# Moving a context's keys and values for the second layer from beside a token layer to beside the experts

## The chip, the cores and the metric

The kernel runs on one core of a Trainium2 chip. The metric is the device time of one execution in microseconds (us), from the first to the last instruction plus a small constant around them. Smaller is better.

## What is computed

Two transformer blocks run one after the other over 256 tokens of width 1024, in 32-bit floats.

The first block is a recurrent and attention mixer, then a mixture of 32 experts (four per token, each expert 1024 x 2048 and 1024 x 1024). The second block has two layers over the same tokens and, beside them, 256 context vectors:

```python
for l in range(2):
    need_ctx = l < 1
    mod, modc = silu(c) @ w_mod[l] + b_mod[l], silu(c_ctx) @ w_mod[l] + b_mod[l]
    sh1, sc1, gt1, sh2, sc2, gt2 = split(mod, 6)          # csh1, csc1, ... from modc
    h  = rms_norm(xl, g_pre_mix[l]) * (1 + sc1) + sh1
    hc = rms_norm(xc, g_pre_mix[l]) * (1 + csc1) + csh1
    ...                      # tokens attend to keys and values of context and tokens
    xl = ...                 # mixer and gated feed-forward of the tokens
    if need_ctx:
        xc = ...             # the same for the context, in layer 0 only
```

So the context passes through layer 0 as a whole (its input does not depend on the first block), and in layer 1 only its keys and values are wanted: a norm, a modulation by `csc1` and `csh1`, and products with two 1024 x 1024 parts of `w_in[1]`.

## The kernel before

**Pieces.** Every weight matrix of a mixer or feed-forward is read in pieces of 128 x 2048 floats (1 MiB). A piece is split into a high and a low part in two halves (`split`, lines 393 and 394: a copy on ScalarE, a subtraction on VectorE), and multiplied in three products: `fm` (lines 414 to 416, weights stationary), `tm` (lines 437 to 439, activations stationary) and `tm2` (lines 463 to 465, two pieces at once). A piece whose inner size is 1024 is 48 matmuls with 256 moving columns. The pieces of `w_f2b` have an inner size of 768 and 36 matmuls each.

**Two paths.** The tokens' path writes its products to the PSUM tiles `ps_a` and `ps_b`, the context's path and the modulations to `ps_c`. Both are Python generators which yield after each piece; `drive(main, side, ratio)` takes `ratio` steps of the side for each step (or credit) that the main yields. This gives the written order. At build a scheduler orders the instructions of each engine anew, except where the code pins them, so the order that runs can differ from the written one. An engine runs its own list in order.

**Stages, in order of time.**
- The first block (`block1`, up to about 360 us), with the modulations as its side: `side_a` reads 1 MiB of modulation weights a step and multiplies (line 484). A modulation has three groups of eight steps; group 0 holds shift and scale of the mixer's norm. `RATIO_A` is the side's share. `hook`, after the merge of the first block, drains that side and begins the context's layer 0.
- The experts (`moe`): 12 sets, first four of four experts ("quads"), then six of two ("pairs"), then two of two ("mixed"). Each set yields 24 times. Its weights come by SyncE's queue into `raw`, its products are lines 1192 and 1217, its results are added by line 1236. The side is the context's layer 0, `CREDIT[n]` steps for each yield of a set with n experts. Its weights come by GpSimd's queue into `rawh`. `CTX_STEPS` counts all steps of that side, and `REST` of them are held back until the experts are done.
- `moe_rest`: the residual and the norm of the tokens. The steps held back (before: the last four pieces, of `w_f2b`) run beside it.
- The tokens' layer 0, with `side_c`: the modulation of layer 1 (24 steps), then `ctx_kv`, which norms the context's result (line 1348 loads it from `xcd` in DRAM, line 540 transposes it), multiplies eight pieces and writes keys and values to DRAM (`spill`).
- The tokens' layer 1, which has no side. Between two stages of a layer, `res_end` adds the residual and gets the factors of the norm (`nrx`), `transposed` (line 540) multiplies by a diagonal `dg`, and `norm_fm` writes `hh` and `hl`, which the next pieces read.

Of the kernel before, what the change touches and what calls it, by code (L numbers as in the profile page):

```python
# [28 lines left out]
for _s in SETS:  # L29
    for _r, _o, _m in _s:  # L30
        CAPS[_r] = _m
CREDIT = {1: 0.0, 2: 0.07, 4: 0.6}
NEG = 1e30
HEADS = 16
CONVW = 31
WINS = (2, 4, 8, 16)
RAW = 6
RATIO_C = 0.36

START_B = 3  # L40
PRE_B = (2, 0, 9)
PRE_C = (8,)
HOLD = 4
RATIO_A = 1.15

CTX_STEPS = 78
REST = 4


# [13 lines left out]
def _kt(h, l):  # L63

    return lambda k: (h[:, k, :], l[:, k, :])
# [147 lines left out]
def drain(gen):  # L213
    for _ in gen:
        pass
# [19 lines left out]
def drive(main, side, ratio):  # L235

    acc = 0.0
    for w in main:
        acc += ratio * w
        while acc >= 1.0:  # L240
            acc -= 1.0
            if next(side, None) is None:
                acc = 0.0
                break
# [60 lines left out]
class _Kernel:  # L305
# [864 lines left out]
    def experts(self, tp, rawp, es, rs, xg, b1, sel, ct, acc, mid=None, first=None):  # L1170
# [9 lines left out]
        parts.reverse()  # L1180
        credit = CREDIT[n]
        aT = tp.tile([128, 8, 128], F32, name="aT", tag="aT", bufs=1)
# [153 lines left out]
    def ctx_kv(self, p, l, x, mod):  # L1336

        A, V, S = self.A, self.V, self.S
        wi = A["w_in2"][l]
        mT = mod["T"][1]  # L1340
        with p.pool(f"kv{l}") as hp:
            Ax = hp.tile([128, 8], F32, name="Akv")
            V.scalar_tensor_tensor(Ax, mT[:, 8:16], 1.0, self.col(f"gpm{l}"), op0=OP.add, op1=OP.mult)
            hh = hp.tile([128, 8, 256], F32R, name="hh4")
            hl = hp.tile([128, 8, 256], F32R, name="hl4")
            with p.pool(f"kvn{l}") as np_:
                xs = np_.tile([128, 2, 1024], F32, name="xc3")
                self.nc.gpsimd.dma_start(xs, x)
                ss = np_.tile([128, 2], F32, name="ssk")
                self.row_ss(np_, xs, ss)  # L1350
                self.rstd_to(ss, ss, 2, 1024)
                self.norm_fm(np_, xs, ss, Ax, mT[:, 0:8], hh, hl)
            yield 1
            act = _kt(hh, hl)
            with p.pool(f"kvs{l}") as kp:
                for ch in range(4):
                    kc = kp.tile([128, 2, 256], F32, name="kc", tag="kc")
                    vc = kp.tile([128, 2, 256], F32, name="vc", tag="vc")
                    self.fm(p, wi[8 + ch], act, 8, lambda _, ps: S.activation(kc, ps, AF.Copy))
                    yield 1  # L1360
                    self.tm(p, wi[12 + ch], act, 8, lambda ps: S.activation(vc, ps, AF.Copy))
                    self.spill(l, ch, kc, vc)
                    yield 1
# [449 lines left out]
    def run(self, out):  # L1813
        nc, A, V = self.nc, self.A, self.V
        cp, dp = self.cp, self.dp
        x = cp.tile([128, 2, 1024], F32, name="x")
        nc.sync.dma_start(x, A["x"].rearrange("(a p) d -> p a d", p=128))
        self.ssx = cp.tile([128, 2], F32, name="ssx")
        self.nrx = cp.tile([128, 2], F32, name="nrx")
        self.modT = cp.tile([128, 48], F32, name="modT")  # L1820
        self.modg = dp.tile([128, 512], F32, name="modg")
        st1 = cp.tile([128, 8, 32], F32, name="st1")
        s1 = self.silu_cols(cp, self.col("c"), 8, "s1")
        V.tensor_copy(st1, s1[:, :, None].to_broadcast([128, 8, 32]))
        st2 = cp.tile([128, 8, 32], F32, name="st2")
        s2 = self.silu_cols(cp, self.col("c2"), 8, "s2")
        V.tensor_copy(st2[:, :, 0:16], s2[:, :, None].to_broadcast([128, 8, 16]))
        s3 = self.silu_cols(cp, self.col("cc2"), 8, "s3")
        V.tensor_copy(st2[:, :, 16:32], s3[:, :, None].to_broadcast([128, 8, 16]))
        mods = []  # L1830
        for l in range(2):
            mods.append(dict(g=dp.tile([128, 512], F32, name=f"mg{l}"),
                             T=[cp.tile([128, 48], F32, name=f"mT{l}{i}") for i in range(2)]))
        self.kvd = [[dp.tile([128, 2, 2, 256], F32, name=f"kvd{l}{ch}") for ch in range(4)] for l in range(2)]
        ctx = A["ctx"].rearrange("(a p) d -> p a d", p=128)

        def mod_steps(l):
            return self.mods(st2, l + 1, A["w_mod"][l], mods[l]["g"], mods[l]["T"], [0, 16])

        b1c = ExitStack()  # L1840
        self.gcols = self.gate_cols(b1c.enter_context(self.px.pool("b1c")))

        xT = self.rawp.tile([128, 2048], F32, name="raw", tag="raw").rearrange("p (k t) -> p k t", k=8)
        with self.px.pool("xn") as np_:
            self.row_ss(np_, x, self.ssx)
            self.rstd_to(self.nrx, self.ssx, 2, 1024)
            self.transposed(np_, x, self.nrx,
                            lambda a, k, pt: self.S.activation(xT[:, k:k + 4, a * 128:(a + 1) * 128], pt, AF.Copy))
        with b1c, self.px.pool("modp", 1) as self.modp:
            drain(self.mods(st1, 0, A["w_ada"], self.modg, [self.modT], [0], (0,)))  # L1850

            def side_a():
                yield from self.mods(st1, 0, A["w_ada"], self.modg, [self.modT], [0], (1, 2))
                yield from mod_steps(0)
            side = side_a()
            xcd = dp.tile([128, 2, 1024], F32, name="xcd")
            cside = _Steps(self.layer(self.pc, 0, ctx, mods[0], True, end=xcd), CTX_STEPS - REST)

            def hook():
                drain(side)  # L1860
                next(cside)
            drive(self.block1(x, xT, hook), side, RATIO_A)

        drive(self.moe(x), cside, 1.0)
        drain(cside)
        g2 = self.gain_row(self.rawp, self.modg, 2, 0, "raw")
        cside.limit = CTX_STEPS
        self.prefetch(self.pc, [A["w_f2b"][0][i] for i in range(4 - REST, 4)])
        self.prefetch(self.px, [A["w_in2"][0][ch] for ch in PRE_C])
        self.moe_rest(x, g2)  # L1870
        drain(cside)

        def side_c():
            yield from mod_steps(1)
            yield from self.ctx_kv(self.pc, 1, xcd, mods[1])
        with self.px.pool("modp2", 1) as self.modp:
            side = side_c()
            main = self.layer(self.px, 0, x, mods[0], False)
            next(main)
            cside.limit += 1  # L1880
            drain(cside)
            drive(main, side, RATIO_C)
            drain(side)
        self.px.score = ["b", "c"]
        drain(self.layer(self.px, 1, x, mods[1], False, end=out.rearrange("o (a p) d -> p (o a) d", p=128)))
# [17 lines left out]
```

## Time and profile before

| | |
|---|---|
| median of 3 runs | 2774.47 us (2771.18 to 2781.82) |
| the profiled execution | 2777.74 us |
| its span, first to last instruction | 2776.0 us |
| TensorE matmul busy | 2596.7 us (94%) |
| VectorE busy | 1442.4 us (52%) |
| ScalarE busy | 1097.5 us (40%) |
| moved by DMA | 790.96 MB, mean 285 GB/s |

The share of busy time is a mean over stages with different limits. Matmuls overlap, so the distance from one start to the next, not the mean duration of one, is what a matmul costs; a busy TensorE in a stretch means that its list was never empty there. A row of a stretch gives its borders (us from the span's start) and its length, then busy us and, in brackets, the number of instructions of TensorE's matmuls, its weight loads, VectorE, ScalarE and GpSimd (left out where there are none), then TensorE's granted clock as a share of the full one, the mean busy share of the 16 DMA engines, and GB/s. A row of the timeline gives start, length, engine, source line, operation, output and inputs, shapes, how many were merged, and in square brackets how long the engine stood idle before and what ended that.

### The profile page before, as it was taken

The numbers are of one execution on the slowest core, as the hardware profiler recorded it, in microseconds if no ns is written. First come the engines' busy times: TensorE is split into PE (matmuls) and PEld (weight loads), VectorE is DVE, ScalarE is ACT, GpSimd is POOL, SyncE is SP. The second block draws the span as 40 slices with busy tenths as digits, with TensorE's granted clock in tenths as the row PEclk, the third lists the DMA queues.
The fourth block names the chain that finished last, engine by engine and source line by source line (L and its number), as shares of the span: only waits on it lengthen the run. The fifth ranks groups of instructions, "written<-read, shape, count | busy, mean of one in ns | idle before, by whom it ended". The sixth has DMA issues, their size and how long they took to land. (4 is left out here: it accounts for less than half of the span.)

```text
span 2776.0 us, 47595 instructions
## 1 busy us (share of the span) xinstructions
PE 2596.7 (94%) x19078; PEld 1971.1 (71%) x19078; DVE 1442.4 (52%) x2413; ACT 1097.5 (40%) x1970; POOL 264.1 (10%) x436
## 2 busy tenths in 40 slices
PE   6999998998998999999898879999999999999998
PEld 4888875666666665553333258779899998899998
DVE  3974566733434333221111158786655658866655
ACT  3663444432323231211100035555543555556443
POOL 1100011112011110000000012210000022200000
PEclk8999999999999999999999989999999999999999
DMA  8768779999999999989999984446666453345452
GB/s 354 263 247 322 274 280 380 363 348 391 395 405 384 404 408 398 373 322 373 390 401 395 391 308 161 157 177 231 251 224 239 166 201 122 122 158 192 152 193 81
DMA packets 154912, 790.96 MB, mean 285 GB/s; under 512 B 17888, under 2 KB 19936, under 8 KB 96064
## 3 DMA queue, kind: packets, MB, share of 16 engines
q1 hardware_dynamic: 131824, 705.30, 66.9%
q0 software_dynamic: 22864, 82.59, 7.8%
q8 instruction: 151, 2.47, 0.3%
q14 instruction: 73, 0.60, 0.1%
HBM read 780.74 MB, written 7.08 MB: 284 GB/s over the span
## 5 line engine op out<-in xcount | busy, mean ns | idle before, releaser
L394 DVE TENSOR_TENSOR wl<-raw,wh 128x1024 fp32r<-128x1024 f32 (+1 forms) x410 | 497.2, 1218 | 293.1 <-ACT wh L393 291.0
L393 ACT ACTIVATE wh<-raw 128x1024 fp32r<-128x1024 f32 (+1 forms) x410 | 425.9, 1046 | 482.8 <-PE ps_a L415 311.4
L414 PE MATMUL ps_a<-hh,wh 128*128 128x256 f32 x1888 | 542.0, 287 | 6.6 <-ACT wh L393 3.1
L416 PE MATMUL ps_a<-hh,wl 128*128 128x256 f32 x1888 | 531.4, 282 | 0.5 <-DVE wl L394 0.5
L415 PE MATMUL ps_a<-hl,wh 128*128 128x256 f32 x1888 | 531.5, 282 | 0.1
L414 PEld LDWEIGHTS ps_a<-hh,wh 128*128 128x128 f32 x1888 | 358.6, 190 | 52.9 <-issue 37.2
L415 PEld LDWEIGHTS ps_a<-hl,wh 128*128 128x128 f32 x1888 | 358.6, 190 | 3.4 <-DVE hl L564 1.2
L416 PEld LDWEIGHTS ps_a<-hh,wl 128*128 128x128 f32 x1888 | 358.4, 190 | 2.9 <-DVE wl L394 2.5
L394 DVE TENSOR_TENSOR wl<-rawh,wh 128x1024 fp32r<-128x1024 f32 x132 | 161.9, 1227 | 320.4 <-ACT wh L393 299.7
L393 ACT ACTIVATE wh<-rawh 128x1024 fp32r<-128x1024 f32 x132 | 139.9, 1060 | 427.8 <-PE ps_c L415 242.0
L414 PE MATMUL ps_c<-hh,wh 128*128 128x256 f32 x832 | 238.4, 286 | 0.0
L416 PE MATMUL ps_c<-hh,wl 128*128 128x256 f32 x832 | 237.2, 285 | 0.0
L415 PE MATMUL ps_c<-hl,wh 128*128 128x256 f32 x832 | 236.8, 285 | 0.0
L1192 PE MATMUL ps_b<-raw,xg 128*32 128x512 f32 (+1 forms) x1152 | 181.4, 610 | 25.9 <-DMA raw<-in_w_dram 25.9
L1192 PE MATMUL ps_a<-raw,xg 128*32 128x512 f32 (+1 forms) x1152 | 184.9, 619 | 18.0 <-DMA raw<-in_w_dram 17.9
L414 PEld LDWEIGHTS ps_c<-hh,wh 128*128 128x128 f32 x832 | 157.8, 190 | 26.3 <-issue 23.4
L416 PEld LDWEIGHTS ps_c<-hh,wl 128*128 128x128 f32 x832 | 157.8, 190 | 16.6 <-issue 15.7
L415 PEld LDWEIGHTS ps_c<-hl,wh 128*128 128x128 f32 x832 | 157.6, 189 | 15.4 <-issue 15.4
L1715 DVE SCALAR_TENSOR_TENSOR wv<-u,cw,wv 128x256 f32<-128x256 f32 x360 | 166.6, 498 | 0.5
L1192 PEld LDWEIGHTS ps_b<-raw,xg 128*32 128x32 f32 (+1 forms) x1152 | 47.1, 120 | 126.2 <-issue 86.3
L1192 PEld LDWEIGHTS ps_a<-raw,xg 128*32 128x32 f32 (+1 forms) x1152 | 48.2, 121 | 121.8 <-issue 91.2
L1217 PE MATMUL ps_b<-raw,aT 128*32 128x512 f32 (+1 forms) x576 | 91.9, 615 | 10.0 <-DMA raw<-in_w_dram 10.0
(524 smaller groups left out, 4815.5 us busy)
## 6 DMA issues: line engine op xcount, KB each, us to landing
raw<-in_w_dram SPq DMA_DIRECT2D x384, 512.0 KB, 12.6
raw<-in_w_dram SPq DMA_DIRECT2D x192, 1024.0 KB, 8.5
raw<-in_w_in_dram SPq DMA_DIRECT2D x96, 1024.0 KB, 4.9
raw<-in_w_mod_dram SPq DMA_DIRECT2D x48, 1024.0 KB, 5.0
raw<-in_w_f_dram SPq DMA_DIRECT2D x44, 1024.0 KB, 4.8
raw<-in_w_ada_dram SPq DMA_DIRECT2D x24, 1024.0 KB, 8.3
rawh<-in_w_in_dram POOLq DMA_DIRECT2D x48, 512.0 KB, 7.6
rawh<-in_w_f_dram POOLq DMA_DIRECT2D x44, 512.0 KB, 7.7
```

The costliest lines, as they stand in the source:

```text
L393: s = self.S.activation(h[:, :n], src, AF.Copy)
L394: self.V.tensor_sub(l[:, :n], src, h[:, :n].bitcast(F32))
L414: self.T.matmul(o, wh[:, w], ah, start=(k == 0), stop=False)
L415: self.T.matmul(o, wh[:, w], al, start=False, stop=False)
L416: self.T.matmul(o, wl[:, w], ah, start=False, stop=(k == kt - 1))
L1192: T.matmul(ps[c], xg[:, k, c], ws[i][:, o:o + 512], start=False, stop=(k == 7), tile_position=(0, c.start))
L1217: T.matmul(py[h][c], aT[:, f, c], ws[i][:, h * 512:(h + 1) * 512], start=(f == 0), stop=(f == 7), tile_position=(0, c.start))
L1715: return V.scalar_tensor_tensor(wk, u[:, f, j:j + 256], cw[:, j * 4 + k:j * 4 + k + 1], wk, op0=OP.mult, op1=OP.add)
```

## The change

The modulation's group 0 of layer 1 is made at the end of the first block's side. The context's chain beside the experts no longer ends with its layer 0 but goes on with `ctx_kv`: 11 more steps, of which two are new yields before the norm. The four steps held back behind the experts are now the last four pieces of keys and values, and `w_f2b` runs beside the experts. Two-expert sets give 0.15 steps a yield for 0.07. The tokens' layer 0 keeps 16 steps of modulation as its side. `RATIO_A` and `RATIO_C` follow the new numbers of steps.

```diff
-CREDIT = {1: 0.0, 2: 0.07, 4: 0.6}
+CREDIT = {1: 0.0, 2: 0.15, 4: 0.6}
-RATIO_C = 0.36
+RATIO_C = 0.25
-RATIO_A = 1.15
-
-CTX_STEPS = 78
+RATIO_A = 1.38
+
+
+CTX_STEPS = 78 + 11
...
                 self.nc.gpsimd.dma_start(xs, x)
+                yield 1
                 ss = np_.tile([128, 2], F32, name="ssk")
                 self.row_ss(np_, xs, ss)
                 self.rstd_to(ss, ss, 2, 1024)
+                yield 1
                 self.norm_fm(np_, xs, ss, Ax, mT[:, 0:8], hh, hl)
...
-        def mod_steps(l):
-            return self.mods(st2, l + 1, A["w_mod"][l], mods[l]["g"], mods[l]["T"], [0, 16])
+        def mod_steps(l, gs=(0, 1, 2)):
+            return self.mods(st2, l + 1, A["w_mod"][l], mods[l]["g"], mods[l]["T"], [0, 16], gs)
...
                 yield from mod_steps(0)
+                yield from mod_steps(1, (0,))
             side = side_a()
             xcd = dp.tile([128, 2, 1024], F32, name="xcd")
-            cside = _Steps(self.layer(self.pc, 0, ctx, mods[0], True, end=xcd), CTX_STEPS - REST)
+
+            def ctx_chain():
+                yield from self.layer(self.pc, 0, ctx, mods[0], True, end=xcd)
+                yield from self.ctx_kv(self.pc, 1, xcd, mods[1])
+            cside = _Steps(ctx_chain(), CTX_STEPS - REST)
...
-        self.prefetch(self.pc, [A["w_f2b"][0][i] for i in range(4 - REST, 4)])
+        self.prefetch(self.pc, [A["w_in2"][1][c + ch] for ch in range(4 - REST // 2, 4) for c in (8, 12)])
...
-        def side_c():
-            yield from mod_steps(1)
-            yield from self.ctx_kv(self.pc, 1, xcd, mods[1])
         with self.px.pool("modp2", 1) as self.modp:
-            side = side_c()
+            side = mod_steps(1, (1, 2))
```

## Rows read from the trace of the kernel before

**Rows 1.** The page: TensorE, DMA share and DMA rate in 40 slices.

```profile
PE   6999998998998999999898879999999999999998
DMA  8768779999999999989999984446666453345452
GB/s 354 263 247 322 274 280 380 363 348 391 395 405 384 404 408 398 373 322 373 390 401 395 391 308 161 157 177 231 251 224 239 166 201 122 122 158 192 152 193 81
```

**Rows 2.** Busy time by stretch: first block, last quad, five sets, token layer 0.

```profile
45.00:300.00 255.00, 252.56 (x1990) 208.93 (x1993) 168.90 (x280) 136.33 (x255) 21.68 (x30) 1.00 0.79 291
...
902.40:1071.00 168.60, 158.08 (x1255) 114.82 (x1253) 64.00 (x74) 50.39 (x65) 19.37 (x36) 1.00 1.03 407
1071.00:1152.10 81.10, 81.10 (x456) 45.05 (x454) 22.78 (x33) 15.35 (x24) 4.97 (x10) 1.00 0.96 376
1152.10:1231.30 79.20, 79.20 (x440) 43.04 (x439) 21.52 (x33) 14.93 (x25) 1.80 (x4) 1.00 0.88 343
1231.30:1299.50 68.20, 61.48 (x285) 24.79 (x283) 11.69 (x23) 7.11 (x16) 0.74 (x2) 0.97 0.90 359
1299.50:1364.40 64.90, 56.74 (x250) 20.94 (x250) 10.31 (x21) 6.51 (x15) 0.74 (x2) 0.97 0.93 377
...
1555.60:1618.70 63.10, 53.07 (x405) 14.99 (x405) 8.10 (x12) 3.46 (x7) 0.00 (x0) 0.95 0.98 390
...
1860.00:2180.00 320.00, 316.66 (x2637) 296.08 (x2636) 191.87 (x250) 160.30 (x241) 6.37 (x9) 1.00 0.62 227
...
2211.20:2253.30 42.10, 40.15 (x324) 39.21 (x323) 27.57 (x45) 23.65 (x39) 14.96 (x29) 0.97 0.78 266
```

**Rows 3.** The same for instructions on `ps_c` alone: the context's matmuls.

```profile
902.40:1071.00 168.60, 103.24 (x812) 97.70 (x810) 8.89 (x13) 5.83 (x10) 1.00 1.03 407
1071.00:1152.10 81.10, 27.73 (x205) 24.99 (x203) 2.75 (x4) 0.58 (x1) 1.00 0.96 376
1152.10:1231.30 79.20, 25.25 (x190) 23.05 (x189) 2.75 (x4) 1.18 (x2) 1.00 0.88 343
1231.30:1299.50 68.20, 4.60 (x35) 4.02 (x33) 0.69 (x1) 0.00 (x0) 0.97 0.90 359
...
2180.00:2211.20 31.20, 11.97 (x98) 11.89 (x98) 0.00 (x0) 1.17 (x2) 1.00 0.64 220
2211.20:2253.30 42.10, 34.76 (x288) 34.28 (x287) 0.00 (x0) 3.50 (x6) 0.97 0.78 266
```

**Rows 4.** Timeline of TensorE: the first transpose of `ctx_kv`'s norm.

```profile
2162.36 1.95 PE L540 MATMUL ps_t<-dg,xc 128*128 128x128 f32 x16
```

**Rows 5.** Timeline of TensorE: two modulation steps in the first block.

```profile
270.84 1.92 PE L484 MATMUL ps_c<-raw,st 128*32 128x512 f32 x16
```

**Rows 6.** Line 1348, the load of the context's result from DRAM.

```profile
DMA to landing us min/median/max: 5.1/5.1/5.1
```

**Rows 7.** Timeline behind the experts: TensorE's longest wait, then GpSimd's last `nrx`.

```profile
1642.38 0.58 PE L465 MATMUL ps_c<-wl,ah 128*128 128x256 f32 x1 [4.67 <-DVE wl L394]
1645.28 0.99 POOL L520 TENSOR_TENSOR nrx<-nrx,pw 128x1 f32<-128x1 f32 x1 [2.27 <-DVE nrx L519]
```

**Rows 8.** Timeline of TensorE: entry to token layer 1, then that layer's middle.

```profile
2245.92 1.95 PE L540 MATMUL ps_t<-dg,x 128*128 128x128 f32 x16
...
2252.70 0.58 PE L414 MATMUL ps_a<-hh,wh 128*128 128x256 f32 x1
...
2576.14 3.75 PE L540 MATMUL ps_t<-dg,x 128*128 128x128 f32 x16 [3.47 <-DVE dg L536]
2580.34 0.55 PE L414 MATMUL ps_a<-hh,wh 128*128 128x256 f32 x1 [0.45 <-DVE hh L563]
```

**Rows 9.** Busy time by stretch: the middle of token layer 1.

```profile
2570.30:2580.30 10.00, 5.96 (x34) 5.35 (x32) 7.68 (x20) 7.03 (x19) 1.52 (x2) 0.75 0.00 0
2580.30:2588.00 7.70, 7.58 (x43) 7.32 (x44) 6.11 (x7) 5.03 (x8) 0.00 (x0) 0.65 0.39 145
```

## The prediction

> **What bounds the kernel now.** I read the page's slices first, then the stretches of busy time cut at the stage borders, then the same cut for the context's matmuls alone, and last the timeline at the borders. The slices [rows 1] show two kernels in one: from the 7th to the 23rd, beside the experts, the DMA rate stands at 322 to 408 GB/s; behind them it falls to 81 to 251 while TensorE stays at 8 or 9 tenths and more. The stretches make this sharper [rows 2]. In the first block TensorE is busy 252.6 of 255 us, in the feed-forward of the tokens' layer 0 316.7 of 320, and around that layer's end 40.2 of 42.1: there each microsecond of matmul work counts. Beside the experts it depends on the set. The last quad carries 812 of the context's matmuls (17 pieces) [rows 3] and runs at 407 GB/s: DMA sets its end. A pair without context work takes 63.8 us (mean of the five sets from 1299.5 to 1618.7; the first 64.9, the last 63.1) at 377 and 390 GB/s, with TensorE idle 8 to 10 us: DMA again. But the first two pairs, with 4.2 and 3.9 pieces, take 81.1 and 79.2 us with TensorE never idle and only 376 and 343 GB/s: there TensorE sets the end. So the change moves matmuls from a stage where they cost all of their time to one where the first of them are cheap and the later ones are not.
>
> **The change, part by part.**
>
> *Out of the tokens' layer 0: keys and values.* The context's 386 matmuls between 2180 and 2253.3 keep TensorE busy 11.97 + 34.76 = 46.7 us [rows 3], 5.85 us for a piece of 48. Their norm's 32 transposes add some 4 us (the first 16 take 1.95) [rows 4]. TensorE is full there, so all 51 us go.
>
> *Out of it too: a third of the modulation.* Two steps take 1.92 us [rows 5], one about 1.0. Layer 0 keeps 16 steps of 24. Of the eight removed some six stood in the full stretch (6 us and 0.6 for the four transposes) and two where TensorE has gaps (half price): 7 us gone; bounds 5 and 9.
>
> *Into the first block: the same eight steps.* TensorE is full, so 8 x 1.0 + 0.6 = 8.6 us. Below, 7.4 (0.93 each); above, 14: the 8.4 MB would take 20.6 us at 407 GB/s if none of it overlapped, but the stage runs at 291 GB/s with a DMA share of 0.79 [rows 2], so I stay near the low end. `RATIO_A` only spreads the 48 steps so that six are left for `hook` (five before); it costs nothing while the full TensorE covers the loads, and 3 us more a step if it doesn't.
>
> *Into the pairs: `w_f2b`, the norm, four of eight pieces.* 144 matmuls of `w_f2b` are three pieces' worth, four pieces come with them, the transposes are 0.75: 7.75 in all. Price of one: at least its bytes, 1.05 MB at 400 GB/s, 2.6 us; at most its matmuls, 5.85. What the trace paid: (81.1 - 63.8) / 4.2 = 4.1 and (79.2 - 63.8) / 3.9 = 3.9, since the first microseconds fill TensorE's idle time. A pair's own matmul work is 56.7 us (busy time of 1299.5 to 1364.4) [rows 2], and 56.7 + 5.85 n gives 81.3 and 79.5 for these two: the rule fits. Where will the pieces fall? The written order gave a pair 24 x 0.07 = 1.7 steps, yet 4 ran, until nothing was left in the third: the order that runs fills TensorE early, and 0.15 (3.6 written steps) won't thin it. So I leave the first two pairs as they are and give the third the three pieces of `w_f2b` (3.7 in all, 78.3 us for 68.2: +10.1). Then the context's residual, the way through DRAM (5.1 us to land [rows 6]) and the norm make a pause, and 4.75 pieces spread over two sets: 2.4 each, 70.7 by the rule; but the third pair, with 0.7 of a piece, ran 4.4 us above a pair without context work, so I take 72: +8.2 each. Sum +26.5. Bounds: 7.75 x 5.85 = +45; and +3.5, if all 16.6 pieces lay evenly over the eight sets (2.1 each, 56.7 + 5.85 x 2.1 = 68.9, times eight 551 for 547.7).
>
> The Trainium skill (DMA: Bandwidth & Descriptors, "Issuing engines are not separate DMA queues") says that transfers started from different engines run on the same 16 DMA engines and interleave, which speaks against the change: the context's weights on GpSimd's queue take their time from the experts'. By that rule alone a piece costs its bytes, and the whole sum below would be 6 us lower. The quad with 17 pieces agrees, at 407 GB/s [rows 2]; the two full pairs, at 376 and 343, show a higher price, so the sum doesn't go by it.
>
> What waits behind the new work: `ctx_kv`'s load stands on GpSimd's queue before the next context weights and the experts' small selection copies; it lands in 5.1 us, and these copies are made a set ahead, so I count nothing. If TensorE's own list holds the norm's transposes too early, experts behind them wait: up to some 10 us, part of the upper bound.
>
> *Behind the experts.* 192 matmuls for 144: +5.9 us at most. Against that, the two last pieces of `w_f2b`, multiplied together, had to wait 4.67 us for VectorE's split amid the residual; their 72 matmuls began at 1642.4 and end at 1651.2 at the earliest, while `nrx` was there at 1646.3 [rows 7], so the tokens' transposes came 5 us or more too late. Single pieces need one split at a time. I take -3, half of what could be saved (bounds -5 and +6).
>
> *The entry to layer 1.* Before, six pieces of keys and values lay between the last product of layer 0 (2211.2) and the transposes at 2245.9, and hid the residual; only 6.8 us passed from the first transpose to the first product [rows 8]. After, nothing is left there. The nearest row is the middle of layer 1, which has no side: 10.0 us from the last product, 2570.3, to the first new one (3.47 of it waiting for `dg`) [rows 8, 9], and behind it the clock: 0.75 and 0.65 in the stretches [rows 9], that is, partly at 1.2 instead of 2.4 GHz; 43 matmuls in 7.7 us, which take 5.2 at 0.122. So 10.0 + 2.5 - 6.8 = +5.7 us; bounds 0 (modulation steps fall into the gap) and +12 (this norm does not take its two halves apart as the middle does).
>
> The rest (names, the two yields, counters) issues nothing.
>
> **Sum.** -51 - 7 + 8.6 + 26.5 - 3 + 5.7 = -20.2 us. From the profiled execution's 2777.7 that is 2757.5; it lay 3.3 us above the median of the runs, so for the median 2754.
>
> **Rivals.**
> *Even spread.* The finer credit lays the pieces evenly over the eight sets: +3.5 for +26.5, so 2731. For it speaks that all eight sets then stay near the DMA's rate; against it, the early filling seen in the first two pairs [rows 3].
> *Full price.* Each piece costs its whole 5.85 us, +45: 2773, no change to speak of. For it: TensorE has no idle time at all in the two full pairs; against it, their 4.0.
> *The chain isn't through.* The context's layer ends too late, and `w_f2b` (17.6 us), the residual and norm (10), DRAM there and back (10.2) and four pieces (23.4) run alone behind the last set: 61 us for the 26.5 they cost beside it, so about 2789, slower. It decides from 34 us uncovered. Also the case in which the change doesn't do what it says. Against it: 22 written steps need 150 of 192 yields at 0.15, and steps ran ahead of the written order.
>
> **Chances.** My forecast 0.55, even spread 0.12, full price 0.24, not through 0.07, 0.02 for what I don't see. A measurement of this kernel tells about 0.5%, 13.9 us, from no change; faster means below 2760.6. Of my forecast 0.47 lies there (a boundary term at its upper end takes it out), with the even spread and the unseen 0.61. Same: 0.08 and 0.22 of the full price, 0.30. Slower: 0.09. The range runs from 2731, the even spread, to 2780, which holds the full price with some microseconds for the first block's DMA; the likeliest case's own range is 2742 to 2768.
>
> **What would show it.** No `ps_c` product but modulation behind 1660; token layer 0 from its first product to its last shorter by some 23 us (the rest of the 58 lay behind its last product); the first block longer by 8 to 9; third pair near 78 us, the next two near 72, the others unchanged; the transposes of layer 0 some 3 us sooner behind the last set; a gap of about 10 us and a clock below 0.8 at the entry to layer 1. Wrong would be a gap beside the experts where TensorE waits for line 540 or `sel`, pairs at 85 us and more, or pieces behind the last set.

## The result and the profile after

The changed kernel takes 2800.68 us (median of 4 runs, 2797.19 to 2802.98) beside 2773.44 for the kernel before on the same chip: ratio 1.0102, 95% interval [1.0079, 1.0124]. It is slower by 28 us where the forecast was 20 faster, and it lies outside the forecast's range. The profiled execution took 2797.19 us, its span is 2795.4, 19.4 above the span before. The profiled execution before lay above its median and the one after is the fastest of its four, so the medians differ by more than the two traces. The terms below are compared trace against trace.

Line numbers: the lines named here stand one further down now (L540 is L541, L484 is L485, L414 is L415, L1348 is L1349).

The page's slices of the changed kernel: TensorE's busy tenths and the DMA rate, which answer to [rows 1].

```profile
PE   6999999998988999999789888999999989999998
GB/s 357 277 248 341 345 209 386 356 345 391 390 403 390 404 409 392 375 360 362 365 396 316 383 403 255 131 154 169 233 203 225 185 148 121 121 152 196 151 196 76
```

The two kernels in one are still there. What changed has to be read at the stage borders. Busy time by stretch of the changed kernel, in the columns of [rows 2]: the first block and its end, the third to the sixth pair of experts, and the entry to the tokens' layer 1 in three parts.

```profile
45.00:300.00 255.00, 247.88 (x1943) 199.57 (x1942) 166.78 (x278) 134.78 (x253) 20.67 (x29) 0.99 0.79 299
300.00:345.00 45.00, 38.99 (x311) 32.31 (x310) 21.68 (x34) 17.91 (x39) 1.75 (x5) 0.96 0.93 368
...
1249.40:1328.10 78.70, 77.95 (x429) 41.77 (x427) 27.11 (x43) 19.12 (x38) 5.89 (x16) 1.00 0.91 358
1328.10:1404.30 76.20, 56.72 (x250) 21.03 (x250) 13.73 (x31) 8.80 (x19) 5.86 (x11) 0.91 0.90 370
1404.30:1472.50 68.20, 61.52 (x296) 25.68 (x296) 14.79 (x29) 12.32 (x31) 0.74 (x2) 1.00 0.94 389
1472.50:1551.60 79.10, 78.32 (x431) 41.64 (x429) 15.21 (x25) 12.93 (x23) 2.95 (x6) 1.00 0.85 328
...
2250.20:2260.20 10.00, 4.01 (x18) 3.51 (x17) 8.00 (x22) 5.63 (x11) 5.01 (x15) 0.74 0.01 2
2260.20:2269.50 9.30, 3.78 (x16) 3.49 (x16) 5.85 (x10) 4.75 (x14) 6.44 (x9) 0.50 0.64 226
2269.50:2279.50 10.00, 9.97 (x62) 10.00 (x63) 2.96 (x4) 2.79 (x5) 0.00 (x0) 0.70 0.29 105
```

The same for the context's products alone (`ps_c`), which answers to [rows 3].

```profile
1249.40:1328.10 78.70, 24.50 (x179) 21.84 (x177) 6.24 (x9) 3.25 (x12) 1.00 0.91 358
1328.10:1404.30 76.20, 0.00 (x0) 0.00 (x0) 0.00 (x0) 0.00 (x0) 0.91 0.90 370
1404.30:1472.50 68.20, 2.00 (x14) 1.78 (x14) 0.00 (x0) 0.00 (x0) 1.00 0.94 389
1472.50:1551.60 79.10, 24.25 (x180) 21.79 (x178) 0.00 (x0) 2.36 (x4) 1.00 0.85 328
```

From such borders comes a ledger, each line the length of a stage in the trace after less that in the trace before, beside the prediction's term. The borders are the first expert product (380.0 before, 394.4 after), the last set's combination (1618.7, 1678.0), the first and the last product of token layer 0 (1661.0 and 2210.9; 1719.6 and 2250.2), and the first of token layer 1 (2252.7, 2269.5).

| stage | predicted | measured |
| --- | --- | --- |
| first block, to the first expert product | +8.6 | +14.4 |
| first expert set and quads | 0 | +3.7 |
| the eight pairs | +26.5 | +41.2 |
| behind the experts | -3 | -0.7 |
| token layer 0, first to last product | -23 | -19.3 |
| entry to layer 1 (41.8 before; 10 forecast, 19.3 measured) | -31.8 | -22.5 |
| layer 1 and the end | +2.5 | +2.6 |
| sum | -20.2 | +19.4 |

No single step failed by 40 us. Four failed by less, all in the same direction: the pairs (14.7), the entry (9.3), the first block (5.8) and token layer 0 (3.7). The quads' 3.7 I don't explain: they took 687 to 696 us in the runs below, with and without the change.

**The fourth pair** carries no context product at all and is 11.3 us longer than before. The timeline of the changed kernel around its longest wait, engine by engine: TensorE, ScalarE, VectorE, GpSimd (start, duration, what runs, and in brackets the idle time before it and what ended it).

```profile
1347.76 3.65 PE L1193 MATMUL ps_a<-raw,xg 128*64 128x512 f32 x16 [2.73 <-DMA raw<-in_w_dram]
1364.50 1.11 PE L1207 MATMUL ps_t<-c_ident,et 128*128 128x128 f32 x4 [13.08 <-DVE et L1204]
...
1357.90 1.06 ACT L528 ACTIVATE nsq<-xc 128x1024 bf16<-128x1024 f32 x1 [29.33 <-DMA xc<-xcd]
1362.40 0.60 ACT L1201 ACTIVATE et<-ps_a 128x512 f32<-128x512 f32 x1 [2.17 <-DVE ps_a L1200]
...
1360.26 0.17 DVE L520 TENSOR_SCALAR ssk<-ssk 128x2 f32<-128x2 f32 x1 [13.48 <-ACT nsq L528]
1361.67 0.69 DVE L1200 TENSOR_SCALAR ps_a<-ps_a 128x512 f32<-128x512 f32 x1
...
1347.13 0.55 POOL L1349 DMA_DIRECT2D xc<-xcd  x1 [8.92 <-DMA xcd<-xc]
```

Read it from the last line up. GpSimd could issue the load of the context's result at 1347.13, once its store had landed. The load landed 10.7 us later, as the view of that load says, which also names who waited for it (5.1 us before [rows 6], beside layer 0's feed-forward, where DMA moved 290 GB/s from 1888 to 1898).

```profile
  ACT nsq L528: 29.3, 1
...
DMA to landing us min/median/max: 10.7/10.7/10.7
```

ScalarE's sum of squares (L528) waits for that load, VectorE's first step of the norm (L520) for ScalarE, and behind L520 in VectorE's list stands L1200, the first step of the expert's activation. TensorE had ended the products of that expert's gate and linear part at 1351.4 and waits 13.08 us for what comes of it. The prediction had looked for this wait only in TensorE's own list and on GpSimd's queue.

The Trainium skill (PSUM — Partial Sum Buffer, "Engine vs sequencer instructions") says that the queues of ScalarE, VectorE and GpSimd are strict first-in, first-out. By that rule L1200 can't pass L520, whatever it needs itself; the trace agrees: VectorE stands idle for 13.48 us in front of L520 and comes to L1200 1.4 us later, with only a step of the same norm (L537) between them.

**The entry to layer 1** is 19.3 us from product to product. The timeline of the changed kernel there: TensorE, VectorE, GpSimd; the last row is the first round of transposes in the middle of layer 1, in the kernel before.

```profile
2255.77 3.78 PE L541 MATMUL ps_t<-dg,x 128*128 128x128 f32 x16 [5.33 <-DVE rr L520]
2260.38 3.78 PE L541 MATMUL ps_t<-dg,x 128*128 128x128 f32 x16 [0.83 <-ACT nf L553]
2269.53 0.55 PE L415 MATMUL ps_a<-hh,wh 128*128 128x256 f32 x1 [5.37 <-DVE hh L564]
...
2258.76 3.48 DVE L395 TENSOR_TENSOR wl<-raw,wh 128x1024 fp32r<-128x1024 f32 x3
2265.57 0.29 DVE L1259 TENSOR_REDUCE lam<-lamt 128x2 f32<-128x128 f32 x1 [3.33 <-POOL lamt L1257]
2265.94 0.76 DVE L564 CAST hh<-nf 128x512 fp32r<-128x512 f32 x2
...
2258.88 3.45 POOL L1269 TENSOR_SCALAR hln<-cols 128x4 f32<-128x4 f32 x1
...
2570.61 2.05 PE L540 MATMUL ps_t<-dg,x 128*128 128x128 f32 x16 [0.16 <-DVE dg L536]
```

Two waits lie one behind the other. The first transposes wait 5.33 us, until VectorE has been through the residual of the second half as well: their diagonal `dg` stands behind it in VectorE's list. Then VectorE splits three weights (3.48 us) and stands idle for 3.33 us until a constant of layer 1 is there (L1259). GpSimd makes it only after its other constants and the issue of the first loads of keys and values, and one of these constants, a product with 4 columns, takes 3.45 us and ends with VectorE's splits; before, at 2224.99, it took 0.21. Only behind L1259 come the casts of the norm, with a fourth split among them, so TensorE waits 5.37 us once more.

The granted clock in the three stretches above is 0.74, 0.50 and 0.70: 0.50 is 1.2 GHz of 2.4 all the way through, after a stretch in which TensorE was busy 4 us of 10. At this clock a round of transposes takes 3.78 us where the covered ones took 1.95 [rows 8]. For the second round that costs nothing: in five of the runs below (keys and values alone, uncovered entry, squares, written share, one load) it is through 1.2 us sooner, the wait behind it is 6.6 us and not 5.37, and the entry is as long.

Layer 1's middle, which I took as the model, waits 0.16 us before its first transposes, since it takes the two halves apart; it has a single split and no constants among its casts, and its last wait is 0.45 [rows 8].

### The profile page after: what moved, and what is told of

Read it like the earlier page. It is cut to its first block, busy times and chain, and to the rows that moved or that the text cites. A ratio compares the mean times of both kernels' runs of the same rounds, so it can differ in the third digit from the quotient of the medians.

```text
span 2795.4 us, 47616 instructions
## 1 busy us (share of the span) xinstructions
PE 2597.2 (93%) x19078; PEld 1972.6 (71%) x19078; DVE 1443.5 (52%) x2413; ACT 1099.2 (39%) x1970; POOL 270.7 (10%) x452
## 5 line engine op out<-in xcount | busy, mean ns | idle before, releaser
L395 DVE TENSOR_TENSOR wl<-raw,wh 128x1024 fp32r<-128x1024 f32 x394 | 479.9, 1224 | 279.8 <-ACT wh L394 274.1
L394 ACT ACTIVATE wh<-raw 128x1024 fp32r<-128x1024 f32 x394 | 410.6, 1051 | 455.9 <-PE ps_a L416 289.1
L415 PE MATMUL ps_a<-hh,wh 128*128 128x256 f32 x1888 | 543.8, 288 | 10.7 <-DVE hh L564 6.7
L415 PEld LDWEIGHTS ps_a<-hh,wh 128*128 128x128 f32 x1888 | 361.5, 191 | 52.6 <-issue 40.6
L395 DVE TENSOR_TENSOR wl<-rawh,wh 128x1024 fp32r<-128x1024 f32 (+1 forms) x148 | 179.3, 1212 | 373.8 <-ACT wh L394 353.5
L394 ACT ACTIVATE wh<-rawh 128x1024 fp32r<-128x1024 f32 (+1 forms) x148 | 154.9, 1049 | 504.8 <-PE ps_c L416 284.8
L415 PE MATMUL ps_c<-hh,wh 128*128 128x256 f32 x832 | 238.0, 286 | 0.0
L415 PEld LDWEIGHTS ps_c<-hh,wh 128*128 128x128 f32 x832 | 156.8, 188 | 28.7 <-issue 24.8
```

The source lines that it names most:

```text
L394: s = self.S.activation(h[:, :n], src, AF.Copy)
L395: self.V.tensor_sub(l[:, :n], src, h[:, :n].bitcast(F32))
L415: self.T.matmul(o, wh[:, w], ah, start=(k == 0), stop=False)
```

## The experiments

The theory after this reading: the change costs in four places that add up, the first block, the held-up fourth pair, the pieces in the pairs, and the uncovered entry. The main rival was the prediction's own account. Ratios are against runs of the kernel before on the same chip: 2775.39 us for the modulation alone, the uncovered entry, the squares and the written share; 2769.26 for the keys and values alone, the one load and the two edits of the entry; 2772.17 for the last two.

**Undoing parts: the modulation alone.** The kernel before, with only the move of eight modulation steps into the first block (and both paces of the change).

```diff
-RATIO_C = 0.36
+RATIO_C = 0.25
...
-RATIO_A = 1.15
+RATIO_A = 1.38
...
                 yield from mod_steps(0)
+                yield from mod_steps(1, (0,))
...
-            yield from mod_steps(1)
+            yield from mod_steps(1, (1, 2))
```

> The kernel before with one part of the change: the eight modulation steps of group 0 move into the first block (share 1.38 there, 0.25 in the tokens' layer 0, so that six pieces still lie at the entry to layer 1). By the prediction's terms +8.6 - 7 = about +2 us, no measurable change. By the profile of the changed kernel, where the first product of the experts comes 14 us later and the tokens' layer 0 is at its 66th piece only 2 us earlier, +12 us, some 2785.

Measured: 2788.55 us, ratio 1.0054 [1.0034, 1.0075]. That is 15 us, half of the whole loss, from eight steps. The first expert product is at 395.5 (380.0 before, 394.4 in the changed kernel). The eight pairs are nearly as before, 549.5 us for 547.7. From token layer 0's first product to layer 1's first pass 584.5 us for 591.7 (seven pieces, not the six expected, cover the entry): the steps that left had cost 7.2 us there, the 7 that were forecast.

**The keys and values alone.** The changed kernel, with all modulation of layer 1 back in token layer 0 and the paces of before. The keys and values are then made with layer 0's modulation, so their values differ.

```diff
-                yield from mod_steps(1, (0,))
...
-                yield from self.ctx_kv(self.pc, 1, xcd, mods[1])
+                yield from self.ctx_kv(self.pc, 1, xcd, mods[0])
...
-            side = mod_steps(1, (1, 2))
+            side = mod_steps(1)
```

> The keys and values beside the experts alone: all modulation of layer 1 stays in token layer 0, and so the keys and values are made with layer 0's modulation (other values, same work). Theory (the parts add: block 1 costs 13, the entry 12, the wait on ScalarE 12): first expert product back at 380, total 2787 to 2791, still slower than before. The prediction's terms (pairs +26.5, layer 0 -51, entry +5.7, no block-1 term): 2751 to 2755.

Measured: 2785.43 us, ratio 1.0059 [1.0038, 1.0079]. The first expert product is back at 377.9, the third to sixth pair take 78.8, 76.2, 69.9 and 79.1, the entry 19.4. So 0.54 and 0.59 per cent stand beside 1.02 for both: within their intervals the two halves add, and each alone makes the kernel slower. The part that was forecast to gain 22 us loses 16.

**The uncovered entry alone.** The kernel before, with a higher pace of its side work, so that all keys and values lie inside token layer 0 and none at its end.

```diff
-RATIO_C = 0.36
+RATIO_C = 0.46
```

> The kernel before with a larger share of the side in the tokens' layer 0 (0.46 for 0.36), so that all eight pieces of keys and values run inside that layer and none is left at the entry to layer 1. Same work, same stage, only the cover of the entry is gone. By the prediction's term +5.7 us, 2779. By the changed kernel's gap of 19.3 us there, for 6.8 before, and a slower clock behind it, +14 us, 2787. If the order that runs still leaves pieces in the gap, 0.

Measured: 2786.82 us, ratio 1.0045 [1.0024, 1.0066]: the same work, no move to the experts, and 12 us slower. The entry's busy time by stretch in this run:

```profile
2241.90:2261.30 19.40, 6.36 (x35) 5.57 (x34) 13.87 (x31) 10.42 (x24) 11.51 (x23) 0.74 0.30 109
```

It is the changed kernel's 19.3 us, with the old order of everything else (at a mean clock of 0.74, for 0.62 over the entry of the changed kernel). The pieces at the end of layer 0 were not waste in a full stretch: they were the cover of 12 us that otherwise stand idle, and the prediction set only 5.7 us against the gain of their 35.

**What in the entry is slow.** Two edits of the changed kernel. First, layer 1's small constants (the reduction of lambda and the products on GpSimd) are made after its norm; `consts` holds the lines that were ahead of it.

```diff
-                V.reduce_sum(lam2, lamt, axis=AX.X)
...
-            G.tensor_scalar(hln[:, 0], self.col(f"lng{l}"), 0.5, None, op0=OP.mult)
...
+            if l == 0:
+                consts()
...
+                if l == 1:
+                    consts()
```

> The changed kernel, with token layer 1's small constants (reduction of lambda on VectorE, five products on GpSimd) made after its first norm and not ahead of it. Theory (this setup stands ahead of the norm's casts in VectorE's list now that nothing covers it): the gap falls from 19.3 to 15 or 16 us, the whole to 2797. Rival (the norm's own chain residual, transposes, casts sets the gap): gap 18.5 to 19.5, total unchanged at 2800 to 2801.

Second, the last eight modulation steps are left to the entry:

```diff
-RATIO_C = 0.25
+RATIO_C = 0.11
```

> The changed kernel, with its last eight modulation steps of token layer 0 placed in the entry to layer 1 (a lower pace of the side work). Theory (the 19.3 us between the layers are idle time of TensorE, since nothing independent is left to put there): the steps fill the gap, layer 0 gets 5 to 8 us shorter, the gap grows by at most 3, and the whole is 2793 to 2797 us beside 2801. Rival (the gap is a chain that the steps' own work on VectorE and in TensorE's list lengthens): gap over 25 us, total 2800 or more.

Measured: 2793.16 us, ratio 1.0082 [1.0063, 1.0101], and 2790.30 us, ratio 1.0073 [1.0054, 1.0093]. Beside the 1.0102 of the change these are gains of 5 and 8 us, and with the intervals of both ratios neither is clear of zero; the traces carry the reading. TensorE's timeline with the constants late:

```profile
2257.06 3.78 PE L541 MATMUL ps_t<-dg,x 128*128 128x128 f32 x16 [5.33 <-DVE rr L520]
2261.67 3.78 PE L541 MATMUL ps_t<-dg,x 128*128 128x128 f32 x16 [0.83 <-ACT nf L553]
2267.03 0.36 PE L415 MATMUL ps_a<-hh,wh 128*128 128x256 f32 x1 [1.57 <-DVE hh L564]
```

The first two waits are untouched, the third falls from 5.37 to 1.57 us and the entry from 19.3 to 15.6. With the modulation steps in it:

```profile
2244.94 5.36 PE L485 MATMUL ps_c<-raw,st 128*32 128x512 f32 x48
...
2255.34 0.66 PE L500 MATMUL ps_t<-c_ident,bmod 128*128 128x128 f32 x4 [0.81 <-DVE bmod L491]
2255.83 1.95 PE L541 MATMUL ps_t<-dg,x 128*128 128x128 f32 x16
2263.52 3.47 PE L541 MATMUL ps_t<-dg,x 128*128 128x128 f32 x16 [5.74 <-ACT nf L553]
2267.72 0.39 PE L415 MATMUL ps_a<-hh,wh 128*128 128x256 f32 x1 [0.73 <-DVE hh L564]
```

The entry grows to 23.0 us, so steps that hold TensorE for 8 us (5.36 for six, some 1.06 for each of two, the transposes) cost 3.7 there. Token layer 0 gets 6.8 us shorter without them (523.8 for 530.6). The mean clock of the entry is 0.93 with the steps in it. What follows the entry is 4.8 us shorter in this trace, but that isn't shown to come from the steps: it lasts 521.1 to 526.8 us in all traces of this document, and the longest is that of a kernel below which has the steps as well.

**The held-up pair.** The changed kernel, with the context's squares summed from the result while it is still on chip, so that no instruction of ScalarE stands behind the way through DRAM.

```diff
+                    if end is not None and own:
+                        self.S.activation(y[:, a, :], xs[:, a, :], AF.Square, accum_out=self.ssk[:, a:a + 1])
...
-                ss = np_.tile([128, 2], F32, name="ssk")
-                self.row_ss(np_, xs, ss)
+                ss = self.ssk
```

> The changed kernel, with the sums of squares for the norm before keys and values taken from the context's result while it is still on the chip, so that ScalarE's list no longer holds an instruction that waits for the way through DRAM. Theory: the fourth pair (76.2 us with no piece in it) falls to some 65 us, and the whole to 2789. Rival: the stall only gives DMA time to run ahead, and the next sets pay it back: 2800, as the changed kernel.

Measured: 2787.56 us, ratio 1.0037 [1.0020, 1.0053]. The third to sixth pair take 78.6, 69.8, 68.1 and 78.7: the fourth alone is shorter, by 6.4 us of its 11.3. TensorE's longest waits of that kernel in the fourth pair:

```profile
1348.29 3.65 PE L1193 MATMUL ps_a<-raw,xg 128*64 128x512 f32 x16 [2.97 <-DMA raw<-in_w_dram]
1354.09 0.66 PE L1207 MATMUL ps_t<-c_ident,et 128*128 128x128 f32 x4 [2.14 <-DVE et L1204]
...
1328.70:1398.50 69.80, 57.48 (x250) 20.71 (x250) 13.72 (x31) 8.75 (x19) 5.83 (x11) 0.98 0.98 404
```

The 13.08 have become 2.14, as long as the same wait lasts in that pair of the kernel before (2.1). The cause is shown. The 4.9 us that remain in that pair are waits for the experts' weights, 7.9 us in all for 3.7 before, at 404 GB/s (last row, the pair by stretch). The pair moves 28.2 MB for 24.5 before, and 3.45 MB of it are on GpSimd's queue, which carried nothing there before: the store and the load of the context's result, 1 MB each, and the first weights behind them. Before, store and load lay behind the experts (at 1665 and 1891 us). This is read from the traces; no run takes these bytes out. The total fell by more than the pair, by 18 us of ratio with some 8 of uncertainty; where the rest lies the traces don't say.

**The written share.** The changed kernel with the old credit of a set of two experts.

```diff
-CREDIT = {1: 0.0, 2: 0.15, 4: 0.6}
+CREDIT = {1: 0.0, 2: 0.07, 4: 0.6}
```

> The changed kernel with the old share of 0.07 for sets of two experts. Theory: where the pieces fall is decided by the order made at build, not by the written share: the first three pairs keep 4.2, 3.9 and 3.7 pieces and the whole stays within 5 us of the changed kernel, 2796 to 2806. Rival: the larger share crowds the pieces; with 0.07 they spread thinner over the eight sets and the whole falls by 10 to 20 us, to 2780 to 2790.

Measured: 2811.79 us, ratio 1.0134 [1.0109, 1.0159], which neither account had expected. The third pair takes 71.0 with 2.2 pieces, the other five 62.8 to 66.5 with none, and the left-over chain stands behind the last set: from its end at 1639.8 to layer 0's first product at 1737.8 pass 98 us for 41.6.

```profile
1639.80:1737.80 98.00, 71.20 (x533) 66.67 (x533) 51.97 (x88) 46.39 (x86) 19.94 (x35) 0.86 0.64 226
```

This is the rival "the chain isn't through", with its price: 56 us behind the set for 40 saved in the pairs, 17 net in these stages of the trace and 9 for the whole by the ratios (1.0134 for 1.0102). So the credit does decide how far the chain gets, and the 0.15 was needed.

**The first block: loads or products?** The changed kernel, whose eight steps all use one loaded tile: the same products, 7 MB of loads left out, other values.

```diff
-            raw = self.load(wsrc[k * 128:(k + 1) * 128, g * 2048:(g + 1) * 2048])
+            if k == 0 or not one:
+                raw = self.load(wsrc[k * 128:(k + 1) * 128, g * 2048:(g + 1) * 2048])
```

> The changed kernel, whose eight modulation steps in the first block all use one loaded tile (the products are the same in number and shape, 7 MB of loads are left out, the values differ). Theory (the first block pays for the 8.4 MB that the steps load): first expert product 394.4 falls to 381 to 386, total 2788 to 2793. Rival (it pays for TensorE's time, as the prediction costed it): first expert product stays within 2 us of 394, total 2798 to 2801.

Measured: 2787.58 us, ratio 1.0068 [1.0047, 1.0088]; the first expert product at 386.5. Its first block by stretch, beside the first two rows of the changed kernel above; the last row is the second stretch in the kernel before:

```profile
45.00:300.00 255.00, 247.88 (x1944) 199.88 (x1943) 166.17 (x278) 134.71 (x253) 20.67 (x29) 0.99 0.80 299
300.00:345.00 45.00, 44.99 (x383) 39.26 (x382) 26.66 (x45) 22.78 (x50) 2.06 (x6) 1.00 0.64 237
...
300.00:345.00 45.00, 41.42 (x336) 36.93 (x329) 31.32 (x55) 27.15 (x56) 3.03 (x7) 0.96 0.69 258
```

To 300 us nothing differs. In the last 45 TensorE's idle time goes from 6.0 us to nothing and the DMA share from 0.93 to 0.64. So 7.9 of the block's cost hang on the loads and 6.5 do not. The steps' own products take what was forecast: up to the first expert product all modulation keeps TensorE busy for 64.8 us in the changed kernel and 56.5 before, 8.3 more for the 8.0 forecast without the transposes. (The 6.5 are not all product time: up to 300 us TensorE idles 7.1 us in both kernels and idled 2.4 before [rows 2], while the side steps come at the higher pace.) How the loads lead to the 6.0 us is not shown: of the waits in that stretch of the changed kernel 0.8 us end with a load, and 3.5 with the split of a weight.

**All mends together, and a different pace in the first block.** The three edits that keep the output (squares, constants, last steps in the entry) in one kernel; and the same with the first block's side work faster, so that fewer of the steps pile up at its end.

```diff
-RATIO_A = 1.38
+RATIO_A = 1.7
```

> The changed kernel with the three mends together: squares summed from the on-chip result, layer 1's constants after its norm, the last eight modulation steps in the entry to layer 1. Theory (the three costs lie at different places and add: -13, -5.5, -7 of the +28, less some overlap in the entry): 0.1 to 0.4 per cent above before, the first expert product still at 394 to 396. Rival (the change gains beyond its mended waits, as the prediction had it): 0.5 per cent or more below before.

> The same, with the side work of the first block at a pace of 1.7 and not 1.38, so that the eight modulation steps are done by the 28th piece and none is left for the end of the block. Theory (the block pays for loads that pile up at its end, where DMA is at 0.93, while 100 to 200 us have 0.57 to 0.70): first expert product falls from 395 to 386 to 391, total 4 to 8 us below the kernel beside it. Rival (the block pays per step, wherever it is put): first expert product 394 to 398, same total.

Measured, over 12 runs each beside 23 of before: 2776.11 us, ratio 1.0013 [1.0001, 1.0026], and 2772.81 us, ratio 1.0002 [0.9989, 1.0016]. The mends take back nearly all the loss, and no more: the best version is level with the kernel before. The faster pace left the first expert product where it was (395.8, against 396.7), as the rival said: its block by stretch shows less idle time in the last 45 us (1.3 for 6.0) and more before them (11.2 for 7.1 from 45 to 300, of that 6.7 in the first 55). It thinned the end and did not clear it: the last step ends at 314 us for 321.

```profile
45.00:100.00 55.00, 48.28 (x334) 37.39 (x333) 29.41 (x37) 25.31 (x40) 7.68 (x9) 0.94 0.90 347
...
300.00:345.00 45.00, 43.74 (x362) 40.59 (x362) 27.47 (x38) 25.69 (x49) 3.27 (x6) 1.00 0.71 273
```

## Why the prediction was wrong

*Out of token layer 0.* The 51 us of keys and values did leave: behind the tokens' first product at 1719.6 no `ps_c` product of layer 0 but modulation is left. But only 16 of them lay in the full stretch before the last product. The other 35 lay in the entry, where "TensorE is full there, so all 51 us go" was true of the row and no measure of the gain: TensorE was full because these pieces covered the residual and the norm. The prediction knew that this cover goes, and priced it too low (below, the entry).

*The modulation's third.* 7 us forecast, and 7.2 in the run with the modulation alone. In the changed kernel token layer 0 became 19.3 us shorter, which leaves 3.3 beside the 16 of keys and values. Some 1.6 of the lack are its first 10 us, which had a granted clock of 0.85 and 73 products, where the kernel before had 1.00 and 86; the rest is open.

*The first block.* The step that failed is "it costs nothing while the full TensorE covers the loads". The upper bound that I set aside, 14 us, is what it cost. The products' part was sized right, 8.3 us for 8.0 (the transposes apart); TensorE was not full once the steps were in, but idle for 8.1 us more than before up to the first expert product (35.5 for 27.4), and 6.0 of that go when seven of the eight loads go. The mean DMA share of 0.79 [rows 2] did not show that, and a finer cut of the kernel before would not have: its last stretch, from 300 to 345, stood at 0.69, and at 0.93 after the change.

*The pairs.* The third pair came as forecast, 78.7 for 78.3. The rule of 56.7 + 5.85 per piece holds again for the sixth, which took 3.7 pieces in one go: 78.3 forecast by it, 79.0 measured. In all 7.75 pieces' worth of work came, as counted (3 in the third, 1.04 with the norm in the fifth, 3.71 in the sixth). But they came bunched and not 2.4 to a pair, so each cost 4.1 us and not 3.4: 5 us. And the pause in the chain was not free for the experts: 11.3 us in the fourth pair, 6.4 of which the squares on chip remove. The list that held the experts up was VectorE's, behind ScalarE's, behind a load. "I count nothing" is the sentence that failed, and it left out bytes too: the way through DRAM had lain behind the experts, and what is left of the 11.3 goes with the 3.45 MB that it and the next weights bring into that pair.

*Behind the experts.* -0.7 for -3: single pieces did remove the wait for the split, and TensorE's idle time there fell from 11.0 to 7.0 us, but the 48 more products took back 3.2 of it.

*The entry.* 10 us forecast from the middle of layer 1, 19.3 measured. With the 2.6 behind it the term is +15 and not +5.7, beyond the far end of its bound (+12). The reason given for that bound came true: this norm doesn't take its two halves apart, 5.33 us before the first transposes for the middle's 0.16. The constants were in no term, and made late they take the entry from 19.3 to 15.6. The middle of a layer was the wrong neighbour: a layer's start also makes constants, splits weights and issues the loads of keys and values, and all of that had been hidden by the same pieces.

*The rivals.* Of the three none came true whole. "Full price" had the size of the pairs' term (+45 for the +41.2 measured) for another reason; "the chain isn't through" is what the old credit would have brought. None gave a sum above before with the chain through, because every term had been allowed to err but only one at a time: all the upper bounds together give -51 - 5 + 14 + 45 + 6 + 12 = +21, about the +19.4 of the traces, if for partly other reasons.

What stays open: the 3.7 us of the quads, how the loads make TensorE idle at the end of the first block, and what a version would take that spreads the pieces at 2 to a pair with the chain still through, which the prediction priced at +3.5 and no run here is.

## What to carry to other kernels

Work that fills TensorE at a stage border is worth the gap that it hides: before moving it out, find what the border looks like without it (here a pace changed by one number showed 19.4 us), and count only the rest as gain. Where a side chain waits for a way through DRAM, look at every in-order list that holds one of its instructions, not only at TensorE's, and take what it needs from the chip before the data leaves. And a DMA share below one is no free place for loads: the first block stood at 0.79 and its last stretch at 0.69, and 7 MB more still cost 7.9 us there.

## What the hardware showed that I had not expected

The same load of the context's result landed in 5.1 us at 290 GB/s [rows 6] and in 10.7 beside the experts, at 370 GB/s over the pair; there the stores of a quarter of that size took as long, 10.4 us.

GpSimd's product with 4 columns (L1269) took 0.21 us before and 3.45 in the entry of the changed kernel, from the start of VectorE's three splits beside it to their end. It stands ahead of the constant that the casts wait for. That the splits cause it was not tried.

Eight steps of matmuls put into the idle entry cost 3.7 us there and left 6.8 in layer 0. The granted clock of the entry was 0.93 with them. Without them it was 0.62 in the changed kernel and 0.74 to 0.81 in five other runs, yet the entry took 19.3 to 19.5 us in all six: its length hung on the waits and not on the clock.
